# Another order for the mixer's steps, and a later place for one row of a norm, in an encoder layer on one core

## The chip, the core and the metric

The kernel runs on one core of a Trainium2 chip. The core has five engines, each with a queue of its own that it works off in order: TensorE (PE, matrix products and transposes), VectorE (DVE, element by element), ScalarE (ACT, element by element and functions), GpSimd (POOL) and SyncE (SP, here only the start of transfers). PE writes to PSUM, eight banks of 128 x 512 floats; everything else lies in SBUF. The metric is the time of one execution on the device in microseconds, lower is better.

## What is computed

One layer of an encoder on x of 512 positions by 1024 channels: a feed-forward half step, a mixer of two parallel parts, and another feed-forward half step, each behind an RMS norm.

```python
x = x + 0.5 * swiglu(rms_norm(x, ffn1_norm), ffn1_w_gate, ffn1_w_up, ffn1_w_down)   # 1024 -> 2752 -> 1024
h = rms_norm(x, mix_norm)
u = h @ w_in                      # 512 Fourier columns | q 8x64 | k 2x64 | v 2x64
f_out = fourier_mixer(u[..., :512], fnet_w, fnet_b)     # real part of a 2-D DFT, then a 128x128 map per group
a_out = gqa_attention(q, k, v, q_norm, k_norm)          # norm of each head, rotation, softmax over 512 keys
x = x + concatenate([f_out, a_out]) @ w_out
x = x + 0.5 * swiglu(rms_norm(x, ffn2_norm), ffn2_w_gate, ffn2_w_up, ffn2_w_down)
y = rms_norm(x, final_norm)
```

## The kernel before

**Numbers in two parts.** Every operand of a product is split into a high part (a cast to float32r, mostly on ACT) and a low part, the difference (`lows`, L130, on DVE). A product of two 128 x 128 x 512 operands is then three matmuls, high by high, high by low and low by high (`product`, L186). So each 512 KB block of weights goes through a transfer into one of three raw buffers (`raw_tile`, L154; the pool `weights` has three), a cast on ACT and a `lows` on DVE, and frees its raw buffer when both are done.

**The feed-forward parts** (`ffn`, run once before and once after the mixer). They start with plain chunks of the gate and up products (`gate`, "gu" in the rows), then go through groups of hidden columns: the products of a seven-product scheme ("r", "q", "p", `seven`), and the down products ("dn", `down`). `prepare` loads and splits the next weights for the seven-product scheme; its pieces are "ring<-s" and "ring<-raw_g" on DVE. In these parts the order on PE and SP is that of the program text; the orders on ACT, DVE and POOL are set by the framework's scheduler when the kernel is built.

**The opening of the first one** (`opening1`). While x and the first weights arrive, four gate chunks are multiplied k by k (`products`, L769), eight k in all. The squares of x are added up in `n0.acc`. At k = 6 `sums()` multiplies them by ones; `mean` (L251, DVE) and `power` (L258, POOL) turn the sums into a column of 1/rms in `n0.r`. `row()` (`Norm.row`, `turn` at L263) transposes this column on PE, four 128 x 128 transposes into a bank "rp", and copies it to SBUF as `rb` (L271, ACT). In the kernel before that happens at k = 7, before the fifth of its twelve matmuls. The chunks are multiplied by this row when they leave PSUM (`evacuate`, L659 to L674), and `operands` (L349, DVE) makes the operands of the seven-product scheme from x and the bank "rp". Behind the opening comes `gate(2 * NF)`, the chunk of the last 64 gate and up columns, whose weights are loaded like any other's, then the other plain chunks.

**The mixer** is cut into 657 named steps. Each step is a Python function that issues its instructions on one engine, and `ORDER` is a list of the names. The list is run inside a region in which all five engines keep the order of the issue, so on each engine the instructions of the steps run in the list's order. Between engines only the data, the banks and the buffers hold a step back. The names that matter here:

- `wk.r`, `wk.h`, `wk.l`: transfer (SP), cast (ACT, L877) and low part (DVE) of a weight block; the same with wq0 to wq3, wv, f0 to f3, fw, and o0 to o7.
- `k.0` to `k.7`, and the same for q0 to q3 and v: eight projection steps of three matmuls each.
- `n1.c`, `n1.m`, `n1.p`: the second norm's sums (PE), means (DVE) and power (POOL).
- for k and q0 to q3: `.sq` squares from the bank (ACT, L906), `.pq` transposes them (PE, L954), `.s0` sums per head (DVE, L959 and L961), `.s1` power (POOL, L965), `.rc` times cosines (DVE, L936 or L934), `.sw` swapped halves (ACT, L919 or L914), `.rs` times sines and added (DVE, L942 and L943). `.sd` swaps halves by transfer for q1 to q3 (SP).
- `kw`, `kp`, `km`: the key's head factors, widened (DVE), transposed (PE), multiplied in (DVE). `k0.0`, `k0.2`, `k1.0`, `k1.2` (ACT, L1018 and L1020) and `k0.1`, `k0.3`, `k1.1`, `k1.3` (DVE): stacked high and low keys. `q0.ah`, `q0.al`, `q0.bh`, `q0.bl`: the same for queries (L976, L985; low parts on DVE).
- `s`, `m`, `e`, `g`, `n`, `t`, `h`, `l`, `v` with three digits (head pair, head, block of 128): scores (PE, two matmuls, L1207 and L1208), maximum (DVE), exponential (ACT), reciprocal sums (DVE, two digits), scaling (ACT), transposes (PE, L1233), high and low parts, values (PE, L1267). The first matmul of `s001` reads `q0.ah`, `q0.al`, `k0.0` and `k0.1`, its second also `k0.2` and `k0.3`.
- `vt`, `vp`, `vs`, `v.h`, `v.l`: the values turned. `f00.0` and so on: the Fourier projection, twelve matmuls of 256 columns each; `map`, `d`, `c`: the transforms; `r`: the attention output split; `y0.0` to `y7.7`: the output projection, `.x`, `.h`, `.l`, `.q`, `.a` what follows from it.

A bank of PSUM goes back to a list when its last reader has been issued, and the next step that needs one takes the oldest. The framework adds every wait that data, banks and buffers need.

Of the kernel before, what the change touches and what calls it, by code (L numbers as in the profile page):

```python
# [18 lines left out]
NF = F // P  # L19
# [27 lines left out]

ORDERED = {getattr(mybir.EngineType, e) for e in ("PE", "DVE", "Activation", "Pool", "SP")}
ORDER = """
wk.r wq2.r wq0.r wq1.r wk.h wk.l wv.r k.0 k.1 wq0.h k.2 wq0.l k.3 wq1.h k.4 k.5 k.6 k.7 n1.c k.sq q0.0 cos  # L50
wq2.h q0.1 k.pq q0.2 q0.3 n1.m k.rc f0.r q0.4 q0.5 k.s0 q0.6 wq2.l k.s1 q0.7 k.sw q0.sq q2.0 wq1.l kw kp wv.h
q0.pq q1.0 k.rs q0.rc q2.1 q1.1 q1.2 q0.s0 q1.3 km q1.4 q0.sw k0.0 wv.l k1.0 q1.5 q1.6 q0.rs q0.ah q0.bh k0.3
q1.7 k0.2 k1.1 q1.sq k1.3 k0.1 q2.2 wq3.r q2.3 q1.sw q0.al q0.s1 k1.2 v.0 q0.bl q2.4 s001 s002 q1.rc s011
wq3.h m001 s010 m011 pos q2.5 s013 v.1 q1.sd q2.6 m010 e011 q2.7 e001 m002 m013 wq3.l s012 e002 s000 e010
e013 v.2 m012 f1.r q2.sq q2.sw v.3 q1.rs f0.h q3.0 v.4 e012 s003 g01 g02 v.5 f3.r m003 q1.ah q1.pq q3.1 v.6
q2.sd m000 q3.2 n002 v.7 q1.bh n001 q1.s0 n012 q1.al e000 e003 q1.s1 q1.bl f1.h s103 n1.p q3.3 g00 q3.4 g03
q2.rc vt n000 q3.5 n003 vp m103 t000 f1.l vs t003 n011 f0.l n010 q3.6 e103 n013 q3.7 t001 h000 h001 t002
q2.rs q3.sw s101 l001 v.h f00.0 l000 f2.r h002 m101 s110 q2.bh s111 l002 v.l f02.0 m111 q2.bl q3.sq f2.h o0.r
f00.1 s100 e101 f00.u m110 m100 e111 t011 g11 q3.sd s112 v000 v001 m112 h003 q2.pq h011 f02.1 l003 l011 v002
s113 s102 q2.ah q2.s0 n101 q2.s1 e100 e110 v003 t010 n111 f02.e h010 m113 t012 q2.al m102 h012 e113 e102  # L60
q3.rc o00.c t013 g13 f03.0 e112 l010 f02.h g10 f2.l f03.1 f01.0 fw.r o1.r n103 n100 v010 s213 l012 q3.pq g12
h013 o00.a q3.rs n102 f01.1 m213 f3.h f01.u q3.s0 v011 s203 v012 l013 t100 e213 fw.h m203 n110 t101 h100 h101
t102 f3.l t103 v013 l100 f10.0 o01.c q3.ah f10.1 f03.e s210 l101 h102 o01.a f03.h e203 s202 n112 l102 g23
q3.bh s212 v100 m210 n113 n203 v101 m212 h103 e210 fw.l q3.s1 m202 f12.0 t113 f02.l f12.1 r0.h l103 f10.u
q3.al s201 t110 v102 s200 v103 o4.r e212 h113 r0.l f12.e f03.l t111 t112 n213 e202 m200 f11.0 h110 o10.c l110
o10.a f13.0 m201 o2.r h111 e200 f12.h e201 g20 s211 q3.bl o0.h g22 o3.r l111 n200 m211 s303 f11.1 e211 m303
f13.1 n202 map1 f11.u v110 o1.h o5.r l113 map0 o0.l h112 f13.e f12.l d00 s313 map0.h v111 g21 l112 e303
map0.l n201 m313 map1.h s301 d01 f13.h d0.h t200 n210 d10 m301 f13.l d11 h200 n212 d1.h v112 t201 d0.l v113
map1.l c0.s l200 h201 o6.r d1.l t203 o11.c l201 t202 c0.c c0.q c1.s o11.a h203 e313 e301 h202 s312 v200 l203
c0.o c1.c m312 v201 n211 l202 s310 s311 c1.q e312 t210 g33 c0.h t213 h210 o2.h d20 d21 d2.h v202 t211 c1.o  # L70
v203 m310 e310 l210 t212 h211 c1.h d30 m311 h212 o2.l s300 n303 d2.l l211 e311 v210 l212 d31 c2.c c0.l h213
v211 m300 l213 d3.h n313 s302 m302 g31 c2.s v212 e300 c1.l v213 y0.0 y2.0 e302 g30 c2.q o21.c d3.l g32 n311
y2.1 n310 n312 c3.s o1.l c2.o c2.h n302 n300 y0.1 y1.0 c3.c o21.a t311 c3.q o7.r o20.c n301 y1.1 t310 c2.l
y0.2 y2.2 h310 y1.2 c3.o t300 c3.h o20.a t302 t301 l310 h300 c3.l l300 h302 v310 y0.3 r1.h l302 h301 h311
l301 v300 y2.3 t312 l311 v301 t303 v311 h303 t313 h312 r1.l l303 l312 v302 h313 y0.4 v303 y0.5 v312 l313 v313
r2.h y1.3 o30.c y1.4 o31.c y2.4 o30.a o31.a r2.l y1.5 y0.6 r3.h r3.l y0.7 y2.5 o5.h y0.x y0.q y1.6 y1.7 y2.6
o5.l y2.7 y1.x y2.x y5.0 o3.h y5.1 o3.l o6.h y5.2 y2.q o6.l y5.3 y5.4 y3.0 y1.h y3.1 y5.5 y3.2 y2.h y1.l y3.3
y1.q y6.0 y5.6 y5.7 y6.1 y3.4 o4.h o4.l y5.x y3.5 y6.2 y3.6 y3.7 y1.a y0.h y4.0 y0.l y3.x y4.1 y6.3 y3.h y5.h
y4.2 y4.3 y2.l y6.4 o7.h y4.4 o7.l y6.5 y4.5 y4.6 y2.a y4.7 y6.6 y7.0 y3.q y6.7 y7.1 y7.2 y3.a y5.q y7.3 y4.x
y4.q y7.4 y3.l y4.a y5.a y5.l y6.x y7.5 y6.q y6.a y7.6 y6.h y7.7 y6.l y4.h y7.x y4.l y7.q y7.a y7.h y7.l  # L80
"""


# [5 lines left out]
def encoder(ctx, tc, A, out):  # L89
# [194 lines left out]
    def ffn(norm, after, wgu, wd, wdt, groups, opening, closing):  # L284
# [6 lines left out]
        with tc.tile_pool(name=f"act{n_}", bufs=1) as ap, tc.tile_pool(name=f"sums{n_}", bufs=2) as sp:  # L291
# [288 lines left out]
            for gi, group in enumerate(groups):  # L580
                last = gi == len(groups) - 1
                ahead = []
                if gi:
                    rest = seven(range(group[0] + 1, min(group[-1] + 2, NF)), ready)
                else:
                    lent = [acts[:, FRONT + i * KD * P : FRONT + (i + 1) * KD * P] for i in range(PLACES - 4, PLACES)]
                    plain.extend(lent)
                    row = []
                    pss = dict(enumerate(opening(gate, lambda: norm.column([norm.acc]), lambda: row.append(norm.row()))))
                    back(lent[:2])  # L590
                    due, parts, left = [*pss, "t"], list(range(KH)), range(2 * len(pss), 2 * n_plain)
                    pss["t"] = [gate(2 * NF)]
                    tail_weights()
                    for i, c in enumerate(left):
                        pss.setdefault(c // 2, []).append(gate(c, by_dma=i in (1,) if n_ else i > 0))
                        if due:
                            j = due.pop(0)
                            evacuate(at[:, place(j)], n_, pss[j], norm)
                        if c % 2 and c != left[-1]:
                            due.append(c // 2)  # L600
                        while len(parts) * len(left) > (len(left) - 1 - i) * KH:
                            o = parts.pop(0)
                            operands(row[0], o, o + 1)
# [12 lines left out]
                waiting, downs = [], []
                for d in range(KD):
                    if last and closing and d == KD - LAST:
                        closing(
                            [(e, down(e, group, gi)) for e in range(d, KD)], residual,  # L620
                            lambda ps, c: by_tokens(ps, c, group), finished,
                        )
                        break
                    if last and d == KD - 2:
                        back(lent)
                    ps = bank(f"dn{n_}_{d}_{gi}")
                    while len(downs) < min(d + 1 + (0 if gi or not n_ else 2), KD):
                        downs.append(down(len(downs), group, gi))
                    steps = downs[d](ps, every)
                    for _ in range(len(group) - (last and d < 2)):  # L630
                        next(steps)
                    waiting.append((d, ps, steps))
                    if d == (1 if gi else 2) and not last:
                        ready = prepare(groups[gi + 1][0] + 1)
                        ahead.extend(ready[1])
                    if d == 0:
                        rest()
                        if last:

# [12 lines left out]
                free.extend(where[j] for j in group)
# [55 lines left out]
    n0, n1 = Norm(0), Norm(1)  # L708
# [12 lines left out]
    def opening1(gate, column, row):  # L721

        pss = [bank(f"gu0_{c}") for c in range(4)]
# [37 lines left out]
        def products(k):  # L761
            hi, lo = ws[k // 2]
            passes = [(c, w, m) for w, m in ((hi, hh), (hi, hl), (lo, hh)) for c in range(4)]
            for n, (c, w, m) in enumerate(passes):
                if (k, n) == (6, 8):
                    sums()
                if (k, n) == (7, 4):
                    row()
                nc.tensor.matmul(  # L769
                    turned(pss[c]), w[:, k % 2, c], turned(m[k]), start=False, stop=k == KD - 1 and w is lo,  # L770
                    skip_group_check=True,
# [829 lines left out]
```

## Time and profile before

| | us |
|---|---|
| three executions | 818.27, 818.72, 1692.98 |
| median | 818.72 |
| the profiled execution | 818.38 |
| its span, first to last instruction | 816.60 |

The profile shows one execution. A row of its timeline has the start, the duration, the engine, the line, the operation, out<-in, the shapes, the count of merged instructions, and in brackets the idle time before it with what ended it. PEld is PE's loading of the standing operand, which runs beside the matmul before. A matmul's duration is drawn longer than its distance to the next one. Rows of several merged instructions have one start and the time to the last one's end.

The first feed-forward part takes the span to about 330 us, the mixer lasts to about 484, the second feed-forward part to the end.

### The profile page before, as it was taken

Reading aid. Unit: us, or ns where it says so; the run is one execution under the profiler, and the core shown is the slowest. Engines: PE = TensorE matmul, PEld = TensorE weight load, DVE = VectorE, ACT = ScalarE, POOL = GpSimd, SP = SyncE. Lnnn points to the kernel's source line nnn. Section 1 sums busy time; section 2 is a strip of 40 time slices with the busy share of each in tenths; the row PEclk is TensorE's granted clock in tenths of the full one; section 3 lists DMA queues with packets and bytes.
Section 4 is the critical chain, followed back from the end, with each engine's and each line's share of the span. In section 5 each row is a group of like instructions: output and inputs, shape, how many; then the busy total and the mean of one; then the engine's idle time right before and its main releaser. Section 6 shows DMA issues by size and latency. Waiting matters only on the chain.

```text
span 816.6 us, 13031 instructions
## 1 busy us (share of the span) xinstructions
PE 809.8 (99%) x4943; PEld 729.3 (89%) x4943; DVE 652.4 (80%) x1083; ACT 503.2 (62%) x871; POOL 67.7 (8%) x75
## 2 busy tenths in 40 slices
PE   9999999999999999999999999999999999999997
PEld 7888998899989998889998888889988998899987
DVE  7997997489856857799998578999955997489674
ACT  7873774267624735699998449557733674267462
POOL 0320000000000000221000003100100000000001
PEclk9999999999999999999999999999999999999999
DMA  7874553345443423442201236554543553345222
GB/s 258 198 172 172 146 132 89 125 130 168 85 151 89 126 67 117 130 149 65 65 26 53 78 109 140 128 188 143 133 116 110 154 145 81 132 130 143 62 78 103
DMA packets 37823, 99.75 MB, mean 122 GB/s; under 512 B 4481, under 2 KB 11265, under 8 KB 37761
## 3 DMA queue, kind: packets, MB, share of 16 engines
q1 hardware_dynamic: 28064, 82.87, 31.2%
q0 software_dynamic: 8832, 15.34, 11.1%
q8 instruction: 38, 0.62, 0.3%
q10 hardware_dynamic: 864, 0.72, 0.3%
q14 instruction: 25, 0.20, 0.1%
HBM read 93.41 MB, written 2.10 MB: 117 GB/s over the span
## 4 chain that ended last, share of the span: by engine, by line
PE 94%; DMA 2%; ACT 1%; DVE 1%; issue 1%; POOL 0%; SPq 0%; POOLq 0%; DVEq 0%; ACTq 0%
PE dn L186 26%; PE r L436 11%; PE mix L186 8%; PE gu L186 8%; PE r L441 8%; PE q L436 4%; PE r L432 4%; PE q L441 4%; PE p L432 4%; PE q L432 4%; PE p L441 2%; PE mix L1267 2%; PE mix L1233 2%; PE mix L1071 1%; PE mix L1072 1%; PE mix L1073 1%
## 5 line engine op out<-in xcount | busy, mean ns | idle before, releaser
L186 PE MATMUL dn<-at,ring 128*128 128x512 f32 x900 | 202.7, 380 | 0.0
L186 PEld LDWEIGHTS dn<-at,ring 128*128 128x128 f32 x900 | 168.0, 188 | 28.9 <-DVE ring L130 0.3
L441 PE MATMUL r<-rt,ring 128*128 128x256 f32 x560 | 154.3, 276 | 0.0
L436 PE MATMUL r<-rt,ring 128*128 128x256 f32 x840 | 147.0, 276 | 0.0
L436 PEld LDWEIGHTS r<-rt,ring 128*128 128x128 f32 x840 | 127.0, 188 | 1.6
L441 PEld LDWEIGHTS r<-rt,ring 128*128 128x128 f32 x560 | 105.1, 188 | 0.2
L391 ACT CAST ring<-s 128x1024 fp32r<-128x1024 f32 x70 | 73.6, 1051 | 35.4 <-PE r L436 16.4
L130 DVE TENSOR_TENSOR ring<-s,ring 128x1024 fp32r<-128x1024 f32 x70 | 85.1, 1216 | 12.6 <-ACT ring L391 10.3
L575 DVE SCALAR_TENSOR_TENSOR gx<-dn,gx 128x512 f32<-128x512 f32 x61 | 41.8, 688 | 63.0 <-PE dn L186 63.0
L172 ACT CAST ring<-raw_dn 128x768 fp32r<-128x768 f32 (+3 forms) x58 | 45.3, 784 | 71.3 <-PE dn L186 55.2
L441 PE MATMUL q<-rt,ring 128*128 128x256 f32 x280 | 77.0, 275 | 0.0
L160 POOL DMA_DIRECT2D ring<-in_wgu x38 | 32.9, 866 | 470.1 <-ACT u L450 372.0
L130 DVE TENSOR_TENSOR ring<-raw_dn,ring 128x768 fp32r<-128x768 f32 (+3 forms) x58 | 51.5, 890 | 9.9 <-ACT ring L172 5.9
L441 PEld LDWEIGHTS q<-rt,ring 128*128 128x128 f32 x280 | 52.6, 188 | 0.0
L130 DVE TENSOR_TENSOR ring<-raw_g,ring 128x1024 fp32r<-128x1024 f32 x35 | 42.6, 1218 | 10.1 <-PE p L432 9.5
L436 PE MATMUL q<-rt,ring 128*128 128x256 f32 x280 | 49.8, 277 | 0.0
L432 PE MATMUL r<-rt,ring 128*128 128x512 f32 x140 | 48.7, 384 | 0.2 <-ACT u L489 0.2
L186 PE MATMUL gu<-ring 128*128 128x512 f32 x216 | 48.9, 381 | 0.0
L432 PE MATMUL q<-rt,ring 128*128 128x512 f32 x140 | 48.3, 382 | 0.0
L432 PE MATMUL p<-rt,ring 128*128 128x512 f32 x140 | 48.3, 382 | 0.0
L186 PEld LDWEIGHTS gu<-ring 128*128 128x128 f32 x216 | 40.4, 188 | 6.9
L391 ACT CAST ring<-raw_g 128x1024 fp32r<-128x1024 f32 x35 | 36.8, 1051 | 15.0 <-DMA raw_g<-in_wgu 12.0
(282 smaller groups left out, 1659.3 us busy)
## 6 DMA issues: line engine op xcount, KB each, us to landing
raw_g<-in_wgu SPq DMA_DIRECT2D x35, 512.0 KB, 3.7
raw_u<-in_wgu SPq DMA_DIRECT2D x35, 512.0 KB, 4.4
raw_dn<-in_wd SPq DMA_DIRECT2D x40, 384.0 KB, 3.2
ring<-in_wgu POOLq DMA_DIRECT2D x35, 256.0 KB, 4.3
raw_gu<-in_wgu SPq DMA_DIRECT2D x12, 512.0 KB, 3.6
raw_o<-in_wo SPq DMA_DIRECT2D x8, 512.0 KB, 3.5
raw_dn<-in_wd SPq DMA_DIRECT2D x8, 448.0 KB, 3.4
raw_wq<-in_wins SPq DMA_DIRECT2D x4, 512.0 KB, 3.6
```

The lines of the kernel that those rows point to most:

```text
L130: nc.vector.tensor_tensor(out=lo, in0=src, in1=asf(hi), op=ALU.subtract)
L160: nc.gpsimd.dma_start(out=lo, in_=src, accum_op=ALU.add)
L172: nc.scalar.copy(hi[:, :n, :], raw[:, :n, :])
L186: nc.tensor.matmul(ps, a, b, start=first and b is mhi and a is whi, stop=last and a is wlo)
L391: nc.scalar.copy(hi, src)
L432: nc.tensor.matmul(turned(ps), whi[:, ks], turned(m), start=start, stop=False, skip_group_check=True)
L436: nc.tensor.matmul(ps[:, t], whi[:, ks], m[:, o * HALF :][:, t], start=start and o == 0, stop=False, skip_group_check=True,)
L441: nc.tensor.matmul(o, wlo[:, ks], m, start=False, stop=stop, skip_group_check=True)
L575: nc.vector.scalar_tensor_tensor(out=x[d][:, t], in0=ps[:, t], scalar=0.5, in1=x[d][:, t], op0=ALU.mult, op1=ALU.add)
L1071: nc.tensor.matmul(ps, hh[k][:, cs], whi[:, a, :], start=k == 0, stop=False)
L1233: nc.tensor.transpose(pts[n][:, c * P : (c + 1) * P], prob[t, b, c][:, kc * P : (kc + 1) * P], ident)
L1267: nc.tensor.matmul(turned(outs[t, b]), w, turned(p), start=kc == 0 and i == 0, stop=kc == 3 and i == 1)
```

## The change

There are two edits. The list `ORDER` is replaced by another one of the same 657 names: no step is added or left out, and the functions behind the names stay as they are. And `row()` of the first norm leaves `products`, where it stood before the fifth matmul of k = 7, and is called in `gate(2 * NF)` before the products of that chunk's k = 1 (where `row` is still empty, which is so in the first feed-forward part alone). Its transposes, its bank and its copy are the same.

```diff
 ORDER = """
-wk.r wq2.r wq0.r wq1.r wk.h wk.l wv.r k.0 k.1 wq0.h k.2 wq0.l k.3 wq1.h k.4 k.5 k.6 k.7 n1.c k.sq q0.0 cos
-wq2.h q0.1 k.pq q0.2 q0.3 n1.m k.rc f0.r q0.4 q0.5 k.s0 q0.6 wq2.l k.s1 q0.7 k.sw q0.sq q2.0 wq1.l kw kp wv.h
-q0.pq q1.0 k.rs q0.rc q2.1 q1.1 q1.2 q0.s0 q1.3 km q1.4 q0.sw k0.0 wv.l k1.0 q1.5 q1.6 q0.rs q0.ah q0.bh k0.3
-q1.7 k0.2 k1.1 q1.sq k1.3 k0.1 q2.2 wq3.r q2.3 q1.sw q0.al q0.s1 k1.2 v.0 q0.bl q2.4 s001 s002 q1.rc s011
-wq3.h m001 s010 m011 pos q2.5 s013 v.1 q1.sd q2.6 m010 e011 q2.7 e001 m002 m013 wq3.l s012 e002 s000 e010
-e013 v.2 m012 f1.r q2.sq q2.sw v.3 q1.rs f0.h q3.0 v.4 e012 s003 g01 g02 v.5 f3.r m003 q1.ah q1.pq q3.1 v.6
-q2.sd m000 q3.2 n002 v.7 q1.bh n001 q1.s0 n012 q1.al e000 e003 q1.s1 q1.bl f1.h s103 n1.p q3.3 g00 q3.4 g03
...
+wq2.r wq0.r wk.r cos wk.h wk.l wq1.r f0.r wv.r k.0 k.1 k.2 k.3 wq0.h k.4 k.5 k.6 wq1.h k.7 n1.c k.sq wq0.l q0.0 wq1.l
+q0.1 k.pq q0.2 q0.3 n1.m q0.4 k.s0 wq2.h k.rc q0.5 q0.6 wq2.l k.sw q0.7 k.s1 q1.0 q1.1 kw wv.h q0.sq k.rs kp q0.rc
+q0.pq q0.sw q1.2 q1.3 wv.l km q0.s0 k0.0 q1.4 q0.rs q1.5 k0.3 q2.0 q0.ah q1.6 k0.1 q0.bh v.0 q0.s1 q0.al q2.1 k1.0
+wq3.r q0.bl q1.7 k1.1 k1.3 k0.2 q1.sq s001 s002 v.1 k1.2 s011 s012 q2.2 s013 m001 q1.sw s003 m002 m012 f1.r m011 e002
+q1.rc e011 e012 m013 q2.3 m003 q2.4 wq3.h v.2 g02 q1.sd q1.rs s000 wq3.l e013 q1.pq q2.5 s010 v.3 e003 q2.6 m010 e001
+m000 n1.p q1.bh g01 q2.7 q1.s0 f0.h q1.s1 v.4 q2.sw e000 q3.0 g03 q3.1 v.5 fw.r q1.ah e010 v.6 n003 v.7 q1.bl q2.sd
+q1.al n012 q2.rc q2.sq vt o0.r n001 f1.h n002 f0.l g00 q3.2 q3.3 n000 q3.4 vp pos q3.5 s103 n013 f1.l q3.6 q3.7 f2.r
...
+v011 m102 v012 g10 f2.l e102 n100 n103 g12 q3.rs q3.pq n102 m213 t102 f03.e n113 t101 v013 q3.bh q3.s0 o00.a f12.0
+h101 n112 t100 h102 l101 m210 f10.0 f3.h h100 l102 q3.ah o01.c f3.l t103 e210 o2.r s203 f03.h fw.h h103 l100 o01.a
+n110 f12.1 s202 f02.l v100 fw.l m202 v101 l103 s212 o1.r f10.1 e202 e213 m212 m203 f10.u t113 q3.bl t110 e212 s211
...
```

```diff
-                    pss["t"] = [gate(2 * NF)]
+                    pss["t"] = [gate(2 * NF, {} if row else {1: lambda: row.append(norm.row())})]
...
                 if (k, n) == (6, 8):
                     sums()
-                if (k, n) == (7, 4):
-                    row()
```

In the second feed-forward part `row()` is called in an earlier chunk as before.

More of the change, by code (lines that the diff above doesn't have):

```diff
@@ L55 @@
-e013 v.2 m012 f1.r q2.sq q2.sw v.3 q1.rs f0.h q3.0 v.4 e012 s003 g01 g02 v.5 f3.r m003 q1.ah q1.pq q3.1 v.6
-q2.sd m000 q3.2 n002 v.7 q1.bh n001 q1.s0 n012 q1.al e000 e003 q1.s1 q1.bl f1.h s103 n1.p q3.3 g00 q3.4 g03
-q2.rc vt n000 q3.5 n003 vp m103 t000 f1.l vs t003 n011 f0.l n010 q3.6 e103 n013 q3.7 t001 h000 h001 t002
-q2.rs q3.sw s101 l001 v.h f00.0 l000 f2.r h002 m101 s110 q2.bh s111 l002 v.l f02.0 m111 q2.bl q3.sq f2.h o0.r
-f00.1 s100 e101 f00.u m110 m100 e111 t011 g11 q3.sd s112 v000 v001 m112 h003 q2.pq h011 f02.1 l003 l011 v002
@@ L60 @@
[L60 to L79, printed above, removed]
@@ L80 @@
-y4.q y7.4 y3.l y4.a y5.a y5.l y6.x y7.5 y6.q y6.a y7.6 y6.h y7.7 y6.l y4.h y7.x y4.l y7.q y7.a y7.h y7.l
+wq2.r wq0.r wk.r cos wk.h wk.l wq1.r f0.r wv.r k.0 k.1 k.2 k.3 wq0.h k.4 k.5 k.6 wq1.h k.7 n1.c k.sq wq0.l q0.0 wq1.l
+q0.1 k.pq q0.2 q0.3 n1.m q0.4 k.s0 wq2.h k.rc q0.5 q0.6 wq2.l k.sw q0.7 k.s1 q1.0 q1.1 kw wv.h q0.sq k.rs kp q0.rc
+q0.pq q0.sw q1.2 q1.3 wv.l km q0.s0 k0.0 q1.4 q0.rs q1.5 k0.3 q2.0 q0.ah q1.6 k0.1 q0.bh v.0 q0.s1 q0.al q2.1 k1.0
+wq3.r q0.bl q1.7 k1.1 k1.3 k0.2 q1.sq s001 s002 v.1 k1.2 s011 s012 q2.2 s013 m001 q1.sw s003 m002 m012 f1.r m011 e002
@@ new lines @@
+q1.rc e011 e012 m013 q2.3 m003 q2.4 wq3.h v.2 g02 q1.sd q1.rs s000 wq3.l e013 q1.pq q2.5 s010 v.3 e003 q2.6 m010 e001
+m000 n1.p q1.bh g01 q2.7 q1.s0 f0.h q1.s1 v.4 q2.sw e000 q3.0 g03 q3.1 v.5 fw.r q1.ah e010 v.6 n003 v.7 q1.bl q2.sd
+q1.al n012 q2.rc q2.sq vt o0.r n001 f1.h n002 f0.l g00 q3.2 q3.3 n000 q3.4 vp pos q3.5 s103 n013 f1.l q3.6 q3.7 f2.r
+n011 t002 t000 q3.sw q2.rs s110 q2.pq m103 q3.sq vs f00.0 q2.ah m110 t001 n010 f00.1 h002 q3.sd h000 q2.s0 h001 s100
+s111 l002 q2.bh l000 l001 v.h f00.u e103 v.l t003 f2.h f02.0 e110 v000 m111 m100 t011 s101 e100 q2.bl e111 v001 t010
@@ new lines @@
+h010 t012 q2.al h003 q3.rc m101 l010 e101 l003 f02.1 s112 f02.e h011 m112 h012 f02.h v002 l012 e112 t013 f3.r v003
+s113 o00.c m113 o3.r f01.0 l011 g11 v010 h013 l013 e113 g13 n101 s213 q2.s1 n111 s102 f01.1 f03.0 s210 f01.u f03.1
+v011 m102 v012 g10 f2.l e102 n100 n103 g12 q3.rs q3.pq n102 m213 t102 f03.e n113 t101 v013 q3.bh q3.s0 o00.a f12.0
+h101 n112 t100 h102 l101 m210 f10.0 f3.h h100 l102 q3.ah o01.c f3.l t103 e210 o2.r s203 f03.h fw.h h103 l100 o01.a
+n110 f12.1 s202 f02.l v100 fw.l m202 v101 l103 s212 o1.r f10.1 e202 e213 m212 m203 f10.u t113 q3.bl t110 e212 s211
@@ new lines @@
+v102 m211 g22 v103 e203 h113 h110 f11.0 f12.e l110 n202 q3.al f12.h t112 t111 s200 v110 f11.1 g23 e211 s201 m200 h111
+o10.c l113 f13.0 e200 f03.l map0 m201 h112 n203 l112 e201 map1 s312 r0.h o0.h map1.h l111 q3.s1 f13.1 o10.a g20 f12.l
+o0.l map0.h f11.u map0.l n213 n200 d10 d00 s301 m312 g21 s303 o4.r f13.e v111 d01 n212 n210 m303 f13.h n201 d0.h d11
+d1.h t200 r0.l map1.l t201 d0.l v112 n211 d1.l f13.l e303 c0.s v113 h201 s313 t202 c0.q m301 h200 h202 l201 l200 t203
+o11.c e301 c0.c m313 v200 l202 e312 e313 v201 o11.a d20 t211 h203 t210 c0.o l203 h211 c1.s l211 s310 c1.q m310 v202
@@ new lines @@
+c0.h t213 o1.h h210 s300 c1.c d21 c0.l e310 c1.o d30 o2.h d2.h s311 t212 d31 l210 m300 e300 d2.l v210 d3.h s302 m311
+h212 o2.l e311 v211 l212 o5.r c1.h m302 v203 y2.0 c1.l g33 c2.s g31 h213 y0.0 o20.c e302 v212 g30 y0.1 d3.l c2.q c2.c
+y2.1 g32 n313 n311 c3.c l213 v213 c2.o n310 c3.s o1.l n312 c3.q t311 o20.a o21.c c2.h t312 c2.l y1.0 n300 y1.1 n301
+c3.o t310 n302 y2.2 n303 y1.2 t300 c3.h h310 o21.a c3.l t302 h300 y0.2 l310 y0.3 y1.3 t301 l300 v310 r1.h h302 r1.l
+r2.h y2.3 h301 l302 v300 y0.4 l301 t303 h311 l311 v301 r2.l h312 h303 v302 l303 y0.5 l312 v311 t313 y0.6 h313 v312
@@ new lines @@
+v303 o30.c l313 v313 o6.r o31.c y1.4 o30.a o31.a y2.4 r3.h y2.5 y1.5 r3.l y1.6 y0.7 o5.h y2.6 y2.7 o5.l y1.7 o3.h y5.0
+y5.1 o3.l o6.h y5.2 y5.3 y5.4 y2.x o6.l y5.5 y3.0 y3.1 y5.6 y3.2 y6.0 y3.3 y1.x y2.h y5.7 y3.4 y3.5 o7.r o4.h y2.l
+y1.q y3.6 y0.x y0.q o4.l y4.0 y3.7 y6.1 y6.2 y4.1 y4.2 y3.x y6.3 y5.x y1.h y0.h y1.a o7.h y4.3 y5.h y4.4 y6.4 y4.5
+y0.l y6.5 o7.l y4.6 y2.q y4.7 y3.q y3.h y2.a y6.6 y7.0 y6.7 y1.l y7.1 y3.a y7.2 y4.x y5.l y7.3 y4.h y4.q y7.4 y6.x
+y5.q y7.5 y7.6 y6.h y7.7 y4.a y5.a y6.q y4.l y6.a y3.l y7.x y7.q y6.l y7.a y7.h y7.l
```

## The prediction, made before the changed kernel ran

> **What bounds the kernel now.** I read the page first: the span and the engines' busy time.
>
> ```profile
> span 816.6 us, 13031 instructions
> ...
> PE 809.8 (99%) x4943; PEld 729.3 (89%) x4943; DVE 652.4 (80%) x1083; ACT 503.2 (62%) x871; POOL 67.7 (8%) x75
> ```
>
> PE is busy for 99% of the span, so no order of the same matmuls can save more than the waits that are left. Those I took from the view of waits for PE's weight-load half, which shows what the matmul row hides behind modelled ends. The columns are total us, times, longest.
>
> ```profile
> PEld rp L263 <- POOL r L258: 1.0, 1, 1.0
> PEld r L432 <- ACT u L489: 0.8, 2, 0.5
> ...
> PEld mix L1207 <- DVE near L130: 0.5, 1, 0.5
> PEld dn L186 <- DVE at L130: 0.4, 1, 0.4
> PEld dn L186 <- DVE ring L130: 0.3, 1, 0.3
> ```
>
> The change reaches two of these: rp (the row of 1/rms) and one mix wait. The other question is what it can make worse, so next came the busy time by stretches (columns: PE, PEld, DVE, ACT, POOL).
>
> ```profile
> 30.00:46.00 16.00, 16.00 (x74) 13.67 (x73) 16.00 (x33) 15.07 (x30) 9.52 (x10) 1.00 0.88 162
> 46.00:58.00 12.00, 12.00 (x56) 10.22 (x56) 11.52 (x21) 9.32 (x16) 1.52 (x2) 1.00 0.79 191
> 58.00:66.00 8.00, 8.00 (x38) 6.84 (x37) 8.00 (x13) 4.03 (x6) 0.00 (x0) 1.00 0.65 168
> ...
> 350.00:400.00 50.00, 49.95 (x319) 44.85 (x318) 47.60 (x100) 46.71 (x91) 6.94 (x4) 1.00 0.29 88
> 400.00:450.00 50.00, 50.00 (x327) 45.10 (x326) 45.69 (x94) 46.65 (x93) 0.00 (x0) 1.00 0.13 43
> ```
>
> DVE is full from 30 to 66 us, just behind the row, and in the mixer's middle DVE and ACT are both over 91% busy beside a full PE. A step that comes late there finds little idle time to make it up.
>
> **The row, gain.** It moves from the middle of the last k step of the opening into the next gate chunk, between its first and second k.
>
> ```profile
> 22.88 2.04 PE L769 MATMUL gu<-ring,at 128*128 128x512 f32 x8
> ...
> 23.94 1.53 POOL L258 TENSOR_TENSOR r<-ms,mhalf 128x4 f32<-128x4 f32 x1 [22.63 <-DVE ms L251]
> ...
> 24.82 1.23 DVE L130 TENSOR_TENSOR ring<-raw_gu,ring 128x1024 fp32r<-128x1024 f32 x1 [0.24 <-ACT ring L172]
> 25.52 0.65 PE L263 MATMUL rp<-ident,r 128*128 128x128 f32 x4 [0.60 <-POOL r L258]
> ...
> 26.83 2.72 DVE L349 SCALAR_TENSOR_TENSOR b<-gx,rp 128x512 f32<-128x512 f32 x4 [0.79 <-ACT rb L271]
> ...
> 27.78 10.72 PE L186 MATMUL gu<-ring 128*128 128x512 f32 x48
> ```
>
> A matmul is drawn 0.38 us long, but 48 take 10.72, so they start (10.72 - 0.38)/47 = 0.22 apart, and a drawn end lies 0.16 behind the next possible start. After the eight matmuls PE could go on at 22.88 + 2.04 - 0.16 = 24.76; the row starts at 25.52, when POOL is done (23.94 + 1.53 = 25.47). Loss: 0.76. In the new place eight more matmuls (1.76) and three of the gate (0.66) come first: 24.76 + 2.42 = 27.18, which is 1.71 after POOL is done. The gate's weights are split by 24.82 + 1.23 = 26.05 at the latest, before its first matmul at 26.52. So all 0.76 goes; the row's four transposes are only moved.
>
> **The row, price.** DVE's first reader follows the row's start by 26.83 - 25.52 = 1.31, so it starts at 27.18 + 1.31 = 28.49, 1.66 later, with nothing of that stage to do before; and PE asks 0.76 earlier. DVE's idle time from 30 to 66 is 0 + 0.48 + 0, so 1.18 of the delay is left there. What is late next are the low parts of down weights:
>
> ```profile
> 62.36 0.55 DVE L130 TENSOR_TENSOR ring<-raw_dn,ring 128x384 fp32r<-128x384 f32 x1
> ...
> 63.86 0.82 PE L186 MATMUL dn<-at,ring 128*128 128x512 f32 x3
> ```
>
> They end at 62.91 and the third matmul of that group needs them, at 63.86 + 0.44 = 64.30: slack 1.39. Afterwards 1.39 - 0.76 - 1.18 = -0.55, a wait of 0.55. Bounds: 0, if the queue for DVE (in this part set by the scheduler, not by hand) puts preparation behind these; 1.66 + 0.76 - 1.39 = 1.03 if no idle time helps. I take 0.55: the second FFN shows the same kind of wait at the same place (0.4 and 0.3, dn on DVE, above).
>
> **The mixer, gain.** The one wait there:
>
> ```profile
> 364.06 0.84 PE L186 MATMUL mix<-ring 128*128 128x512 f32 x3
> ...
> 364.94 0.19 PEld L1207 LDWEIGHTS mix<-ks,near 128*128 128x128 f32 x1 [0.48 <-DVE near L130]
> ...
> 365.27 0.38 PE L1208 MATMUL mix<-ks,near 128*128 128x512 f32 x1
> ```
>
> Step s103 waits for q1.al. PE could have started it at 364.06 + 0.84 - 0.16 = 364.74 and its second matmul at 364.96, which came at 365.27: 0.31 lost. The old list has no PE step between q1.al and s103; the new one has q3.2, q3.3, q3.4, vp and q3.5, four times 0.66 and 0.44 = 3.08 us. The 0.31 goes.
>
> **The mixer, price: the opening.** The new list starts the scores (s001) sooner: three projection steps fewer stand ahead of it (11 of q1, q2 and v after q0.7, not 14), 3 x 0.66 = 1.98. Their inputs come later:
>
> ```profile
> 337.04 0.75 DVE L936 SCALAR_TENSOR_TENSOR rot_k<-mix,qkg,cos 128x512 f32<-128x512 f32 x1
> 337.16 0.60 PE L954 MATMUL mix<-ident,sq_k 128*128 128x128 f32 x4
> ...
> 337.80 0.69 DVE L959 TENSOR_REDUCE sc<-mix 128x8 f32<-128x512 f32 x1
> 337.82 2.76 ACT L919 ACTIVATE sw_k<-mix,qkg 32x512 f32<-32x512 f32 x4 [0.70 <-DVE rot_k L936]
> 338.52 0.17 DVE L961 TENSOR_TENSOR sc<-sc,eps_ms 128x8 f32<-128x8 f32 x1
> ...
> 342.00 0.60 ACT L906 ACTIVATE sq_q<-mix 128x512 f32<-128x512 f32 x1 [1.42 <-PE mix L186]
> ...
> 342.63 1.05 ACT L877 CAST ring<-raw_wv 128x1024 fp32r<-128x1024 f32 x1
> ...
> 343.07 0.74 DVE L936 SCALAR_TENSOR_TENSOR rot_q<-mix,qkg,cos 128x512 f32<-128x512 f32 x1
> ...
> 343.85 2.76 ACT L919 ACTIVATE sw_q<-mix,qkg 32x512 f32<-32x512 f32 x4 [0.17 <-DVE rot_q L936]
> ```
>
> and after it, down to the first scores:
>
> ```profile
> 346.64 0.69 DVE L942 TENSOR_TENSOR sw_q<-sw_q,sin 128x512 f32<-128x512 f32 x1 [0.29 <-ACT sw_q L919]
> ...
> 347.37 0.69 DVE L943 TENSOR_TENSOR rot_q<-rot_q,sw_q 128x512 f32<-128x512 f32 x1
> 347.98 2.78 DVE L130 TENSOR_TENSOR ks<-rot_k,ks 64x512 fp32r<-64x512 f32 x4
> 348.09 0.62 ACT L976 CAST near<-rot_q 64x512 fp32r<-64x512 f32 x1 [0.20 <-DVE rot_q L943]
> ...
> 349.38 0.62 ACT L1020 CAST ks<-rot_k 64x512 fp32r<-64x512 f32 x1
> ...
> 351.99 0.40 PE L1207 MATMUL mix<-ks,near 128*128 128x512 f32 x1
> ```
>
> In the new list k.rc stands behind k.s0 on DVE: k.s0 cannot start before 337.80 (its transposes), so k.rc runs 338.61 to 339.36 and k.sw (ACT), which waits for k.rc in the trace, 339.39 to 342.15. Then wv.h, now ahead of q0.sq, 342.06 to 343.11, and q0.sq to 343.62, 1.02 later than before. q0.pq, one projection step later than its 342.93 by the trace's order, waits some 0.1. Next q0.rc to 344.39, q0.sw to 347.18 (before: 346.61), q0.rs to 348.63. From there ACT does q0.ah, q0.bh, k1.0 and only then k0.2, four casts of 0.62 with 0.02 between: k0.2 ends at 351.20. DVE does k0.3, k0.1 and q0.al in 3 x 0.695 from 348.55: 350.63.
> PE would reach s001 at 351.99 - 1.98 = 350.01, and its second matmul, which reads what k0.2 writes, at 350.23; with 0.05 from one engine to the next (25.47 to 25.52 above) that one now starts at 351.25: 1.02 late, the wait at q0.pq within it. I take **1.0**. The next doubtful step, s011, needs k1.3, done at 350.63 + 3 x 0.7 = 352.73; its second matmul comes at 351.25 + 0.22 + 0.44 (s002) + 0.66 (v.1) + 0.22 = 352.79, in time. Bounds: 0, if ACT gets ahead of this walk, and 3.3 (rival three).
> The row behind the size is ACT's wait for DVE's read of the same bank (0.70 and 0.17). [...]
>
> A load of a weight block, from issue to landing (last column, us):
>
> ```profile
> raw_wv<-in_wins SPq DMA_DIRECT2D x1, 512.0 KB, 3.8
> ```
>
> **Other moved steps at nothing.** SP: cos and sin move ahead of wq1, so they are not later than before. fw.r and o0.r are loaded early and hold two of the three raw buffers, so f3.r waits for f2.l; from f2.l to f12.1, which needs f3, a load (3.8), a cast (1.05) and a low part (1.23) take 6.1. The list has seven PE steps of 0.44 and two of twelve half-width matmuls (12 x 0.11) there, 5.7 in all. If DVE does f2.l no earlier than its place in the list, 0.4 is bare; DVE has mostly run ahead of its place here (one wait for it in the mixer), so I take nothing and leave 0.4 to the range. POOL: the three loads of pos move behind two powers, n1.p and q1.s1; their readers, map and d, stand some 190 list steps on. At the end of the mixer DVE does more just before y7.x, but only y7.l is needed at once, and that by the last k of the next gate chunk, seven k steps of 0.66 on. The tail stays.
>
> **Sum**, against the profiled execution (818.38: span 816.60 and 1.78 around it; the median of the runs shown is 818.72, so 0.34 above): 818.38 - 0.76 + 0.55 - 0.31 + 1.0 = 818.86.
>
> **Rivals.** One: everything is covered; ACT and DVE get ahead in the opening, the scheduler puts down weights first. Then 818.38 - 0.76 - 0.31 = 817.31. For it: the old order, with its tight places, shows one wait only. Against it: the walk above is a chain of rows without a gap to give. Two: one of the two prices is paid, 817.86 (down weights alone) or 818.31 (opening alone).
> Three, the other side: wv's load is late. The new list puts f0.r ahead of wv.r, and both wait for raw buffers. If wv.r gets that of wq1 (split before 336) it lands in time. If it gets that of wq2, whose split now follows k.rc and ends near 340.5, it lands 3.8 later at 344.3, wv.h starts 2.3 behind 342.06, and all of q0 with it: 1.0 + 2.3 = 3.3 and 818.38 - 0.76 + 0.55 - 0.31 + 3.3 = 821.16. It decides from an issue after 338.3. In the old list wv.r stands ahead of f0.r.
>
> **How the numbers follow.** Chances: the sum, 818.9, 0.45, rival one 0.25, two 0.20, three 0.10. The range goes from rival one less 0.3 (the runs shown lie 818.27 to 818.72), 817.0, to rival three, 821.2; my own case alone is 818.3 to 819.7 (the down weights at 0 and at 1.03, and the median's 0.34). A change of 2%, 16 us, is what counts as told from none; all cases lie within 3 us, so within 2% has 0.97, faster 0.01 and slower 0.02, for what no row shows.
>
> **What would show it.** Right: the wait rp on POOL is gone; a wait of mix L1207 or L1208 on ACT ks or DVE near, 0.5 to 1.0, stands near 350; the cast of raw_wv comes before sq_q; sw_q ends about 0.6 later than 346.61; s103's wait is gone; a dn wait on DVE ring appears between 60 and 68. Wrong: no wait near 350 (rival one), a wait of ACT for raw_wv (three), or a new wait between 370 and 450, which I have not priced.

## The result, and the profile after

| | before | after |
|---|---|---|
| median, us (the runs beside each other) | 819.12 | 827.31 |
| lowest and highest | 818.27 to 819.52 | 826.88 to 827.94 |
| the profiled execution, its span | 818.38, 816.6 | 827.94, 826.2 |

The ratio is 1.0106, interval 1.0090 to 1.0122: 8 us slower, where 818.9 and at most 821.2 were forecast. (The 1692.98 of before belongs to these runs too: it counts in the median of before, not in its lowest and highest.) In the changed kernel's text the line numbers are smaller by 2 (feed-forward) and 4 (mixer) than before; in the experiments they shift in the same way by one or a few.

The page first:

```profile
span 826.2 us, 13031 instructions
...
PE 814.4 (99%) x4943; PEld 729.7 (88%) x4943; DVE 653.2 (79%) x1083; ACT 502.8 (61%) x871; POOL 66.9 (8%) x75
```

The instructions are the same 13031. PE's drawn busy time went up by 4.6 though its work did not change, so a busy share says little here. I measured PE's loss from the starts in the trace instead: for each matmul the time to the next start, less the most frequent such time in these traces for a matmul of its width (220 ns for 512 columns, 113 for 256, 109 for 128; the few other widths likewise). These sums are called the **excess** below. Over the whole execution it is 8.4 us before and 17.9 after, a difference of 9.5, as large as that of the spans (9.6). By stretch (the mixer's are counted from its first product, since the kernels reach it at different times):

| excess, us | 22 to 30 | 55 to 75 | mixer, 0 to 32 | 32 to 68 | 68 to 172 |
|---|---|---|---|---|---|
| before | 0.85 | 0.01 | 0.52 | 0.72 | 1.07 |
| after | 0.07 | 5.38 | 3.63 | 0.75 | 2.92 |

The view of waits of PE's weight loads names what stood in the way (total, times, longest):

```profile
PEld dn L184 <- DVE at L128: 3.4, 3, 2.4
...
PEld mix L950 <- ACT sq_q L902: 1.6, 1, 1.6
PEld dn L184 <- ACT at L170: 1.2, 1, 1.2
PEld mix L950 <- ACT sq_k L902: 1.1, 1, 1.1
...
PEld mix L1203 <- DVE near L128: 0.7, 1, 0.7
...
PEld mix L1204 <- ACT ks L1016: 0.4, 1, 0.4
```

The wait of rp on POOL is gone. In its place stand waits for down weights (dn, 3.4 and 1.2; all but 0.5 of it in the first feed-forward part), two waits for squares in the opening of the mixer, and the predicted wait at s001.

**The first feed-forward part.** ScalarE's timeline after, around the row and then in the mixer's opening (start, duration):

```profile
24.29 1.05 ACT L170 CAST ring<-raw_gu 128x1024 fp32r<-128x1024 f32 x1 [0.23 <-DVE wt L128]
28.07 1.05 ACT L170 CAST at<-raw_gu 128x1024 fp32r<-128x1024 f32 x1 [2.74 <-DMA raw_gu<-in_wgu]
29.15 1.06 ACT L157 ACTIVATE at<-at 128x1024 fp32r<-128x1024 f32 x1
30.12 0.57 ACT L269 COPY rb<-rp 128x512 f32<-128x512 f32 x1
...
341.13 1.05 ACT L873 CAST more<-raw_wq 128x1024 fp32r<-128x1024 f32 x1 [4.18 <-DMA raw_wq<-in_wins]
342.09 0.59 ACT L902 ACTIVATE sq_k<-mix 128x512 f32<-128x512 f32 x1
...
348.72 1.05 ACT L873 CAST ring<-raw_wv 128x1024 fp32r<-128x1024 f32 x1
349.79 0.60 ACT L902 ACTIVATE sq_q<-mix 128x512 f32<-128x512 f32 x1
```

The row's transposes run at 27.35, 0.17 from the predicted 27.18. But its copy `rb` has slipped behind the cast of the next chunk's weights (chunk 5, at<-raw_gu), and that cast waits 2.74 for its load. In the kernel before, the copy stood ahead of it:

```profile
26.21 0.59 ACT L271 COPY rb<-rp 128x512 f32<-128x512 f32 x1 [1.42 <-PE rp L263]
...
27.36 1.05 ACT L172 CAST at<-raw_gu 128x1024 fp32r<-128x1024 f32 x1 [0.56 <-PE gu L769]
```

After the change VectorE waits for the copy:

```profile
30.71 0.69 DVE L657 TENSOR_TENSOR g0p<-gu,rb 128x512 f32<-128x512 f32 x1 [4.13 <-ACT rb L269]
...
31.92 1.40 DVE L347 SCALAR_TENSOR_TENSOR b<-gx,rp 128x512 f32<-128x512 f32 x2
```

Its first reader is 3.88 later than before, not 1.66, and it is another one: the first evacuation, with the multiplications for b behind it (31.92, where before they came first, at 26.83). The tiles b share their buffers (tag "raw_g") with the loads raw_g, and those stand ahead of the down weights in SP's queue. SP's own timeline, after:

```profile
56.20 0.33 SPq L381 DMA_DIRECT2D raw_g<-in_wgu  x1
...
57.11 8.59 SPq L152 DMA_DIRECT2D raw_dn<-in_wd  x5
...
334.97 0.33 SPq L1339 DMA_DIRECT2D cos<-in_cos  x1
...
335.88 0.38 SPq L152 DMA_DIRECT2D raw_wq<-in_wins  x1
```

and before:

```profile
50.27 0.33 SPq L383 DMA_DIRECT2D raw_g<-in_wgu  x1
...
51.16 12.10 SPq L154 DMA_DIRECT2D raw_dn<-in_wd  x5
...
316.15 12.64 SPq L154 DMA_DIRECT2D raw_wq<-in_wins  x3
...
332.80 0.42 SPq L1343 DMA_DIRECT2D cos<-in_cos  x1
```

The down weights are issued 5.95 later. PE runs into them from 55 us on: 3.7 us of waits, and then eight matmuls that each take 0.207 longer, 1.65. The stretches show why (PE, PEld, DVE, ACT, POOL, then the granted clock, the DMA share and GB/s):

```profile
60.00:64.00 4.00, 2.17 (x9) 1.18 (x7) 3.96 (x7) 3.08 (x6) 0.62 (x1) 1.00 0.32 112
64.00:68.00 4.00, 3.14 (x8) 2.52 (x9) 4.00 (x8) 1.47 (x2) 0.29 (x1) 0.65 0.92 190
68.00:72.00 4.00, 4.00 (x18) 3.32 (x18) 3.75 (x5) 2.28 (x3) 0.00 (x0) 0.93 0.97 350
```

The granted clock of the second row, 0.65, is a mean: in the trace's clock record it is 1.00 up to 65.2, 0.50 for the next 3.4 us and 1.00 from there to 822.9. The eight matmuls start within those 3.4 us, and 0.22 + 0.207 is nearly twice the usual distance.

**The mixer.** The SP rows above show the other cause. `cos` is now ahead of wq1's load. It is issued at 334.97, 0.19 after the mixer's first product (334.78), and wq1's load only behind it, at 335.88. Before, the third raw_wq load went out at 316.15 + 12.64 - 0.33 = 328.46, 1.66 ahead of the first product (330.12). So ACT waits 4.18 for raw_wq, the squares of k stand behind that cast, and what follows from them (k.pq, k.sw, wv.h, q0.sq) moves back link by link.

### The profile page after: what moved, and what is told of

Read it like the earlier page. It is cut to its first block, busy times and chain, and to the rows that moved or that the text cites. A ratio compares the mean times of both kernels' runs of the same rounds, so it can differ in the third digit from the quotient of the medians.

```text
span 826.2 us, 13031 instructions
## 1 busy us (share of the span) xinstructions
PE 814.4 (99%) x4943; PEld 729.7 (88%) x4943; DVE 653.2 (79%) x1083; ACT 502.8 (61%) x871; POOL 66.9 (8%) x75
## 4 chain that ended last, share of the span: by engine, by line
PE 86%; DVE 4%; DMA 4%; ACT 3%; issue 2%; POOL 1%; SPq 1%; DVEq 0%; POOLq 0%; ACTq 0%
PE dn L184 25%; PE r L434 12%; PE r L439 8%; PE mix L184 6%; PE gu L184 4%; PE q L434 4%; PE q L439 4%; PE r L430 4%; PE p L430 4%; PE q L430 4%; PE p L439 2%; PE mix L1263 1%; PE mix L1229 1%; PE mix L1126 1%; PE mix L1204 1%
```

## The experiments

Times are medians, each beside runs of the kernel before on the same chip. "Old" and "new" are the two lists.

**One edit at a time.** The row alone (old list, the second diff of the change):

> Only the row moves; the mixer keeps its old order. Theory A (the row costs by what now stands ahead of its copy: ScalarE copies 1/rms behind a weight cast that waits for its load, VectorE's first reader starts about 3.9 us later, the down weights' loads stand behind it on SP): about +4.6 us of before, 823 to 825, with dn waits on the down weights of some 3 us between 55 and 63 us and a granted clock below 0.95 in the slices right behind them. Rival (all of the loss is the mixer's, the row is worth what was predicted for it): 818.0 to 819.5. The wait for r on POOL near 25 us is gone in both.

Measured: 823.87 against 819.72, ratio 1.0054 (1.0039 to 1.0069). The new list alone, row at the old place:

> Only the mixer's order changes; the row stays at its old place. Theory A (cos waits for space of the first FFN at the head of SP, the loads of wq1 and of all steps behind it wait with it): about +4 us of before, 822 to 824, with the square sq_k waited for near 341 and sq_q near 350. Rival (the mixer's loss is a late echo of the late first FFN): 818.3 to 819.5, no wait on sq_k.

Measured: 824.12, 1.0059 (1.0044 to 1.0074). So the loss comes from both edits in nearly equal parts, 4.2 and 4.4, together 8.6 against the 8.2 of the whole. The mixer's excess of the row alone is that of before in every stretch (table at the end), and that of the list alone is 0.01 at 55 to 75: neither loss is an echo of the other.

**The row.** Four matmuls later only, still in the opening:

```diff
-                if (k, n) == (7, 4):
+                if (k, n) == (7, 8):
```

> Before with the row four matmuls later in the same k step (behind the eighth of twelve instead of the fourth); the old mixer order. Theory A: the wait for r on POOL (0.6 to 0.76) goes, the copy of 1/rms comes under 1 us later, but a weight cast now stands ahead of it on ScalarE: 818 to 820, worse than before only if that cast waits for its load. Rival (each us of delay of the first reader returns as a wait for down weights): 819 to 820. If neither: 818.0 to 818.4, a gain of 0.7.

Measured: 819.54, 1.0001 (0.9991 to 1.0010). It still waits 0.5 for POOL, and 0.8 comes back at 55 to 75: the copy again has the cast ahead of it. The time alone fits both theories. Then I pinned the copy ahead of a cast, with an order edge in the framework:

```diff
-            nc.scalar.copy(self.rb[:, t], ps[:, t])
+            self.copied = nc.scalar.copy(self.rb[:, t], ps[:, t]).ins
...
-                        pss.setdefault(c // 2, []).append(gate(c, by_dma=i in (1,) if n_ else i > 0))
+                        with tc.issue_after(norm.copied) if i == 0 and not n_ else nullcontext():
+                            pss.setdefault(c // 2, []).append(gate(c, by_dma=i in (1,) if n_ else i > 0))
```

> The row at its new place, with one order added: ScalarE's copy of 1/rms stands ahead of the cast of the fifth chunk's weights, as it did before; the old mixer order. If it is the cast ahead of the copy that costs: the copy starts near 27.9, VectorE's first reader near 28.5, 1.7 later than before instead of 3.9; the wait for r (0.76) is gone, the dn waits are 0 to 0.6 and the clock stays full: 0.8 less to 0.2 less than before. Rival, the place itself costs (1.7 later sends the loads of the down weights as late as 3.9 does): dn waits of 2 to 3 and 821 to 824.

Measured: 824.7, 1.0064 (1.0049 to 1.0079). This edge hit the wrong chunk: i = 0 is chunk 4, whose cast PE needs early, and chunk 5's cast stayed ahead of the copy. It says nothing of either theory, but shows what a late weight costs there:

```profile
PEld gu L187 <- DVE ring L131: 4.2, 1, 4.2
```

With `i == 1` it is chunk 5's cast that waits:

> The row at its new place, and ScalarE's copy of 1/rms ahead of the cast of chunk 5's weights (at), where it stood before; VectorE still takes the first evacuation (L659, L660 of before) ahead of the four multiplications that make b. If the cast ahead of the copy is what costs: first reader near 28.5 instead of 30.9, the loads of the down weights 2 to 3 us earlier than in the row alone, dn waits of 0 to 1 and a full clock: 818.7 to 820. Rival (VectorE's new order, b behind the evacuations, keeps the loads late): dn waits of over 2, 821 to 824.

Measured: 820.24, 1.0008 (0.9999 to 1.0017). Most of the loss is gone; one wait is left, because VectorE evacuates before it makes b:

```profile
PEld dn L187 <- DVE at L131: 1.4, 1, 1.4
```

Last, VectorE's order too. The two multiplications that make each b become a function `scaled(rp, i)`, called for the first two b ahead of the first evacuation, which an edge keeps behind them:

```diff
+                            if i == 0 and not n_:
+                                scaled(row[0], 0)
+                                after_b = tc.issue_after(scaled(row[0], 1))
+                            else:
+                                after_b = nullcontext()
-                            evacuate(at[:, place(j)], n_, pss[j], norm)
+                            with after_b:
+                                evacuate(at[:, place(j)], n_, pss[j], norm)
```

> The same, and VectorE's order of before as well: the four multiplications that make b ahead of the first evacuation. So only the 1.7 us of the new place are left, which the prediction priced at 0.55 behind a gain of 0.76: first reader near 28.5, wait for r gone, dn waits 0 to 1.0, 0.8 less to 0.3 more than before. Rival (the place itself costs, whatever the order): dn waits of over 2, 821 or more.

Measured: 818.70 against 819.42, 0.9991 (0.9982 to 1.0000), the row at the new place and the order of before behind it. ScalarE and VectorE there:

```profile
28.76 0.59 ACT L272 COPY rb<-rp 128x512 f32<-128x512 f32 x1 [3.32 <-PE rp L264]
29.24 1.05 ACT L173 CAST at<-raw_gu 128x1024 fp32r<-128x1024 f32 x1
```

```profile
29.38 2.72 DVE L351 SCALAR_TENSOR_TENSOR b<-gx,rp 128x512 f32<-128x512 f32 x4 [2.68 <-ACT rb L272]
```

This execution's start lost 0.93 more than the one of before (excess up to 22 us: 2.82 against 1.89), so the reader is at 28.45 on the old clock: the predicted 28.49. The excess at 55 to 75 is 0.01, with no wait for down weights. The down weights are still issued later than before here, at 54.16 or 53.23 on the old clock, against 51.16: these 2.1 are covered. With the copy alone ahead they came 2.9 later and 1.33 was lost, in the changed kernel 5.95 later and 5.4. The later place itself costs nothing. The order behind it was the whole loss, and it was two orders: ScalarE's copy and VectorE's b.

**cos.** The new list with `cos` behind wq1's load:

```diff
-wq2.r wq0.r wk.r cos wk.h wk.l wq1.r f0.r
+wq2.r wq0.r wk.r wk.h wk.l wq1.r cos f0.r
```

> The new order of the mixer with one step put elsewhere: cos behind wq1's load; the row at its old place. Theory A: wq1's load is issued about 1.8 us before the first product again, the wait on sq_k (1.1) goes and the chain behind it is 1 to 2 us earlier; what stays is the opening's own loss (0 to 1.0) and the gain of s103 (0.3): 818.3 to 820.5. Rival (the order of k.rc, k.s0 and wv.h on VectorE and ScalarE is the cause, not SP): as with the new order alone, 822 to 824.

Measured: 822.31, 1.0036 (1.0023 to 1.0049), 1.8 below the new list alone, which lies between the two forecasts: `cos` is one cause, and most of the list's loss is left. The mixer's excess falls from 7.29 to 5.27. What is left at the opening is mostly the predicted wait at s001:

```profile
PEld mix L1205 <- DVE near L128: 0.7, 1, 0.7
...
PEld mix L1206 <- ACT ks L1018: 0.4, 1, 0.4
PEld mix L952 <- ACT sq_q L904: 0.3, 1, 0.3
```

The old list with `cos` ahead of wq1's load, nothing else:

> Before with one step moved: cos's load ahead of wq1's; nothing else. Theory A (SP is held by cos until the first FFN's last tiles are free, and wq1's load behind it starts only after the first product): a wait on sq_k near 341 to 343 and on what follows from it, 1 to 3 above before. Rival (a late wq1 alone is covered in the old order, whose wq1.h is two products earlier): within 0.5 of before.

Measured: 820.20 against 819.43, 1.0011 (1.0002 to 1.0021), between the two forecasts again: 0.8 lost, less than half of what `cos` costs in the new list, but with the same wait:

```profile
PEld mix L954 <- ACT sq_k L906: 1.4, 1, 1.4
```

The issue times against the mixer's first product tell the mechanism. The load of cos goes out 0.19 after that product in every kernel of the new list, and in the old one with cos first: after (334.97 and 334.78), the old list with cos first (331.71 and 331.52), the new list alone (330.90 and 330.71) and with cos later (331.16 and 330.97). In these traces SP's wait for it ends on PE's down products (dn) of the first feed-forward part: 9.9 us of waiting in the first three, 1.5 with cos later. So it is held until that part has ended. That what it waits for is that part's space in SBUF, which its tile takes over, is read from the code and was not tried. wq1's load goes out 1.1 after the product when it stands behind cos, and 1.65 before it when it stands ahead.

**The rest of the new list.** Old steps up to number 48, then the new list:

> The new mixer order behind the first 48 steps of the old one (through q0.rc: the loads, k.rc ahead of k.s0, wv's cast behind q0.sq), row at the old place. If the waits after 350 are the opening's: against the version with cos later, the 1.0 at 350 to 360 goes and the time is 1 to 3 below its 822.3, at 819.3 to 821.3; the waits from 400 to 500 (2.9 with cos later, 1.0 before) shrink with it if they are its echo. Rival, the new order is itself too tight on VectorE and ScalarE from 350 to 500: 821.5 to 822.5, those waits stay.

Measured: 821.54, 1.0026 (1.0015 to 1.0037). Old up to 74:

> As the kernel with the old opening, but the first 74 steps are the old ones (the whole of q0 and the first of q1, q2, k0 and k1). If the waits of 350 to 360 come from the steps between 48 and 74, they go only here; the waits of 400 to 500 stay if the rest of the new order makes them (1.5 to 2 above before: 820.5 to 822) and go if they are an echo of a late start (819 to 820).

Measured: 822.05, 1.0029 (1.0017 to 1.0042). The old opening takes away 0.8 of the 1.27 (excess 1.79 against 0.52), but nothing behind it: 68 to 172 keeps 3.1 against 1.07, so that is no echo. The old steps from 48 to 74 change neither (1.05 at 0 to 32, 3.1 at 68 to 172). I cut the lists further back, at 440 and at 491:

> The mixer's first 440 steps in the old order, the rest in the new one; the row at its old place. If the 1.2 at 400 to 460 of the new order (over before) is made by its own steps there, it goes: excess from 340 to 460 as before, and what is left is 460 to 500 (0.7 to 0.9) and nothing behind it: 819.4 to 820.6. Rival (the losses at 400 to 500 come from steps behind the 440th): 821 to 822, as with the first 74 old.

> The mixer's first 491 steps old, the rest new; the cut lies where the two orders have all but three steps in common, so that it makes few waits of its own (the cut at 440 made 3). Row at the old place. If the loss at 400 to 440 is made by the new steps there and the one at 460 to 500 by those behind step 491 (raw_o's last loads and the sums of squares later): 400 to 460 as before (0.9), 460 to 500 stays at 0.9 or so against 0.1: 820.0 to 820.6. Rival (one loss, handed on): nothing left, 819.0 to 819.7.

> The counterpart: the kernel with the old opening (48 old steps, then the new order) up to step 491, and the old order behind it. If the losses are local: 400 to 440 stays 1 to 1.5 above before, 460 to 500 goes to 0.1 to 0.3: 820.5 to 821 (0.8 below the kernel with the old opening). Rival (a loss handed on to the end): 821.5.

Measured: 824.92 (1.0062, 1.0046 to 1.0077), 820.59 (1.0014, 1.0004 to 1.0023) and 821.25 (1.0021, 1.0012 to 1.0031). The cut at 440 made waits of 1.6 and 1.4 of its own and did not answer. The cut at 491, where the lists differ by three steps, did. (The third run has the first 48 old steps too, then the new ones up to 491.) Old first, new behind:

```profile
PEld ss L244 <- issue: 0.6, 1, 0.6
PEld mix L186 <- DVE more L130: 0.4, 2, 0.2
```

New first, old behind:

```profile
PEld mix L1233 <- DVE oo L1282: 0.6, 1, 0.6
PEld mix L1130 <- ACT e L1221: 0.5, 1, 0.5
```

The third run's 821.25 lies between its two forecasts, but the stretches tell the two apart. They are local losses: 68 to 100 us into the mixer has 1.44 with the new steps and 0.66 with the old, 130 to 172 has 0.61 with the new steps behind the cut and 0.09 with the old. (Between them, near the cut, both mixtures lose 0.5 to 0.9 more than the old list.) Which moved step makes each small wait stays open.

**Together.** Both repairs on the changed kernel, and the row's repair on the old list with one step moved (s103 behind q3.3, the gain that the new list had):

> The changed kernel with both repairs: cos's load behind wq1's, and the row at its new place with the copy of 1/rms and b in the order of before. If the parts add: the time of the order with cos later (822.3, or 2.6 to 2.9 above before) less the row's 0.7: 1.9 to 2.2 above before, 821.3 to 821.8, so the rest of the new order costs more than its gain. Rival (what is left over in the mixer comes from the first FFN's state): 819 to 820.5.

> The same with one step of the old mixer order moved, s103 behind q3.3: its wait of 0.3 near 364 goes if nothing else moves: 0.3 below the kernel with copy and b first. Rival (the matmuls that wait for s103's scores then wait): the same time or 0.3 above.

Measured: 821.96 (1.0030, 1.0020 to 1.0040), a little above the 821.3 to 821.8 that follow if the parts add. The row's part is as repaired (0.01 at 55 to 75), but the mixer's excess is 0.8 above that of cos later alone (6.05 against 5.27), and no run shows why. Either way the rest of the new list loses more than both gains bring. The last one measured 818.20 against 819.42, 0.9984 (0.9975 to 0.9993), which is faster than before by more than its interval, though by 1.2 us only.

| excess, us | 22 to 30 | 55 to 75 | mixer, 0 to 32 | 32 to 68 | 68 to 172 |
|---|---|---|---|---|---|
| row alone | 0.05 | 6.34 | 0.52 | 0.73 | 1.07 |
| new list alone | 1.11 | 0.01 | 2.86 | 1.05 | 3.37 |
| new list, cos later | 1.09 | 0.02 | 1.79 | 0.50 | 2.98 |
| old to 48, then new | 0.79 | 0.01 | 0.97 | 0.55 | 3.13 |
| old list, cos first | 1.20 | 0.00 | 1.47 | 0.99 | 1.04 |
| copy ahead of chunk 5 | 0.06 | 1.33 | 0.52 | 0.73 | 1.07 |
| copy and b first | 0.06 | 0.01 | 0.52 | 0.73 | 1.07 |
| the same, s103 later | 0.05 | 0.01 | 0.52 | 0.45 | 1.07 |

## Why the prediction was wrong, step by step

- *Row, gain, 0.76*: right. The excess at 22 to 30 fell by 0.78.
- *Row, price, 0.55*: wrong. The step that failed is "DVE's first reader follows the row's start by 26.83 - 25.52 = 1.31, so it starts at 27.18 + 1.31 = 28.49". It carried ScalarE's and VectorE's order over unchanged, in a part where the scheduler sets it. With that order kept by hand the reader does come at 28.45 and the price is 0, not 0.55 but within its bounds. As the kernel was built, the copy fell behind a cast that waits for a load, and b behind the evacuation: 5.4.
- *Mixer, gain, 0.31*: right as a mechanism. Moving s103 alone took 0.28 off 32 to 68. That stretch reads 0.50 in the new list with cos later too, against 0.72 before; in the changed kernel it reads 0.75, the gain hidden by what comes late there.
- *Mixer, price, the opening, 1.0*: right in place and size. With cos out of the way the stretch from 19 to 32 us behind the first product has 1.10 against 0.20, at s001's two matmuls, as forecast. ScalarE's waits for VectorE ahead of sw, 0.70 (k) and 0.17 (q0) before, stand in the trace after as well: sw_k waits 2.33 for rot_k and sw_q 0.82 for rot_q.
- *Other moved steps at nothing*: this is where the mixer's forecast failed: "SP: cos and sin move ahead of wq1, so they are not later than before." It asked only when cos comes, not what stands behind it on SP. Held until the first feed-forward part had ended, cos put wq1's load from 1.66 ahead of the first product to 1.10 behind it, and that cost 2.0.
- *The rest of the list*, also at nothing: 1.9 at 68 to 172. The text named a new wait between 370 and 450 as what would prove it wrong, and had not walked that part. Which moved steps make these waits is open. In stretches where DVE and ACT are over 91% busy, nothing was not a safe price.
- Rival three (wv's load late) was right about the load and not about the wait. It is issued at 343.47, or 8.69 after the first product (before: 332.43, 2.31 after), which is 338.81 if counted from the old first product, and past the 338.3 named. But ACT comes to its cast later still (348.72, no wait), ahead of sq_q as forecast. The load that ACT did wait for was wq1's.

The sum by what was measured: 818.38 - 0.78 + 5.37 + 2.0 + 0.9 + 1.9 = 827.8, against the 827.94 of the profiled execution. The terms of the mixer come from the experiments; its gain (0.2) and the rest of the opening's excess (0.4) are left out and nearly cancel.

## What to carry to other kernels

Where a scheduler sets an engine's order, a moved instruction may come back at another place in the order of its readers: look at what now stands ahead of it on each engine, and pin the order with an edge if the old one was good. When a transfer moves up in an in-order queue, ask when its destination becomes free and price everything that is now behind it. Price a reordered list stretch by stretch where the engines are full, since many waits of 0.2 to 0.6 add up.

## What the hardware showed that was not expected

The granted clock fell to half in one long wait (3.9 us with the edge on chunk 4), and also behind two shorter ones with matmuls between them. With the cut at 440, PE waited 1.6 and 1.1 (excess of two matmuls) within 4 us, with two matmuls of a score between:

```profile
428.00:432.00 4.00, 1.62 (x9) 0.88 (x8) 2.53 (x7) 2.01 (x5) 0.00 (x0) 1.00 0.00 0
432.00:436.00 4.00, 4.00 (x18) 3.76 (x19) 3.93 (x9) 1.02 (x3) 0.00 (x0) 0.57 0.00 0
436.00:440.00 4.00, 4.00 (x21) 3.42 (x20) 3.12 (x8) 3.95 (x8) 0.00 (x0) 1.00 0.38 131
```

In the kernel with the copy ahead of chunk 5, one wait (an excess of 1.2) left it at full speed:

```profile
60.00:64.00 4.00, 2.98 (x14) 2.21 (x13) 4.00 (x9) 1.44 (x4) 0.92 (x1) 1.00 0.57 109
64.00:68.00 4.00, 4.00 (x19) 3.40 (x19) 3.94 (x7) 2.21 (x3) 0.00 (x0) 1.00 0.90 284
```

These stretches of 4 us are cut by hand, so that 0.65 and 0.57 are means. The clock record in the traces of before and of the changed kernel holds only 1.00 and 0.50, and the times between its changes are whole multiples of 3.413 us, up to the fall at the end: 237 of them before, 18, 1 and 221 in the changed kernel. The clock is at half for 3.4 us in the changed kernel (from 65.2) and with the cut at 440 (from 432.0), and for 6.8 with the row alone (from 64.5) and with the edge on chunk 4 (from 36.2). In the 3.41 us ahead of these four falls PE is drawn busy for 1.07, 1.02, 1.41 and 0.55. Of the steps of 3.41 at full speed without a fall behind them, the two that lost most have 2.07 (new list alone, from 342.9) and 2.08 (changed kernel, from 348.5).

So the waits ahead of these falls cost more than their length: 3.7 us of waits brought 1.65 more in the changed kernel, and 2.6 more with the row alone. In the changed kernel's 3.413 us at half the matmuls of 512 columns start 0.427 us apart, against 0.220 at full speed. What decides whether a wait brings a fall was not shown.
